# Two output projections with other banks and another written order, token statistics first, rotation tables on VectorE, in a two-layer hybrid decoder trunk

## The chip, the core and the metric

The kernel runs on one core of a Trainium2 chip. The core has TensorE (matmuls, which write to the eight banks of PSUM), VectorE, ScalarE and GpSimd, each with an instruction queue of its own that it works off in order, and SyncE (SP), whose queue issues the DMA transfers. GpSimd does not touch PSUM in this kernel. The metric is the device time of one execution in microseconds, the median of the runs. All arithmetic is on the device; the host only lays out the weights and transposes the activations.

## The reference

Input `x` has 1024 tokens of width 1024; there are two layers, each a mixer with a residual and a gated MLP with a residual. Cut to what matters:

```python
def reference(x, ...):
    h = x
    for layer in range(2):
        hn = rms_norm(h, mix_norm_g[layer])
        h = h + (even_mixer if layer == 0 else odd_mixer)(hn, ...)
        h = h + conv_ffn(rms_norm(h, ffn_norm_g[layer]), ...)
    return h

def even_mixer(hn, w_in, q_gain, k_gain, ret_gain, w_out):
    sb_q, sb_k, sb_v, r_q, r_k, r_v, r_g = split(hn @ w_in)
    out_a = stick_breaking_attention(rms_norm(heads(sb_q), q_gain), rms_norm(heads(sb_k), k_gain), heads(sb_v))
    ret = retention_chunkwise(rope(heads(r_q)), rope(heads(r_k)), heads(r_v))
    out_b = from_heads(rms_norm(ret, ret_gain)) * silu(r_g)
    return concatenate([out_a, out_b]) @ w_out

def odd_mixer(hn, w_in, w_alpha, b_alpha, out_gain, w_out):
    g_q, g_k, g_v, g_r, g_a = split(hn @ w_in)
    o = gla_chunked(g_q, g_k, g_v, log_sigmoid(g_a @ w_alpha + b_alpha) / 16)
    return (from_heads(rms_norm(o, out_gain)) * silu(g_r)) @ w_out
```

## The kernel before

Activations are kept transposed: eight tiles of 128 features x 1024 tokens. Every float32 operand of a large matmul is split into a high part (a ScalarE cast to the type that TensorE takes, `hi`) and a low part (the rest, `lo`, a subtraction on VectorE or GpSimd), and a product is three matmuls: hi x hi, hi x lo, lo x hi.

**Start.** `norm_end` makes 1/rms of the tokens from the sums of squares: twice as rows (`pn`, `self.rstd`, 512 tokens each, in the PSUM banks `st` and `O`) and once by token (`pt`, `self.rstd_tok`, 8 columns, in the bank `st`), each time with `rsqrt` (two ScalarE and three VectorE steps; L206 to L210). The first projection (queries and keys of the first head pair) and the values run meanwhile on TensorE; `sb_qk` scales them by the tokens' 1/rms, transposes them into the bank `st` (L587) and splits them (`split`, L541 and L546). The rotation tables `cos` and `sin` are loaded and multiplied by 1/rms on GpSimd (L895, L896).

**Even mixer.** Four rounds `p` of attention over head pairs are woven with projection units (`weave`, `work`): the next pair's queries and keys, a raw gate, values. `work` loads and splits the weight parts of a unit, part of them ahead during the unit before. VectorE, ScalarE and GpSimd keep the written order there (`manual_schedule`); TensorE's order, and that of any engine not named, is made by the framework's planner from its own costs. `issue_after(i)` keeps instructions behind instruction `i` of their engine.

**Output projections.** Each multiplies the concatenated heads `cat` (eight tiles) by a 1024 x 1024 matrix with Winograd's form of Strassen's scheme: for two blocks `p` of output features at a time, seven products, run in the order 1, 2, 3, 6, 7, 5, 4, each of 2 blocks x 4 tiles `c` x 3 matmuls = 24 matmuls of 128x512. After the first two blocks (with all the preparation of the right operands) come the other two blocks, another seven products with the right operands kept. The left operands are made from the weights by `out_left` in that order (11, 12, 12', s2, 21, 11', 22): sums on GpSimd (L294), cast on ScalarE (L71), subtraction (L73). The right operands 1, 2 and 3 are blocks of `cat` (`out_hi` L361, `out_lo` L367, the latter on GpSimd); 6, 7, 5 and 4 are mixes that `out_sums` makes tile by tile in two PSUM banks (a copy L440, two VectorE steps, a cast each L437 and a subtraction each L438, two VectorE steps more, again casts and subtractions). `out_group` runs the products into PSUM pairs `x`, `y`, `w`, `z` and adds them to the residual on VectorE (`sums`, L479).

In the even projection the last tile of `cat` is the gated one: `gate` multiplies a raw gate product by 1/rms, applies Silu, and multiplies tile 7 (L816 to L820). In the odd one, the last four gate blocks are the last seven products of `project_pair` (12 matmuls each, L1016 to L1018); `gla_gates` finishes each with three exponentials and logarithms, and `end()` (L1402) multiplies the result into `cat`.

Of the kernel before, what the change touches and what calls it, by code (L numbers as in the profile page):

```python
# [11 lines left out]
F32 = mybir.dt.float32  # L12
# [15 lines left out]
class Trunk:  # L28
# [219 lines left out]
    def norm_end(self, tok, second="O", parts=None):  # L248
        nc = self.nc
        self.rstd = self.cp.tile([P, T], F32, tag="rstd", name="rstd", bufs=1)  # L250
# [15 lines left out]
        if tok:  # L266
            ps = self.stat("pt")
            for tb in range(NC):
                nc.tensor.matmul(ps[:, tb:tb + 1], self.ssum[tb // 4][:, tb % 4 * P:(tb % 4 + 1) * P],
                                 self.ones_d[:, 0:1], start=True, stop=True)  # L270
            self.rstd_tok = self.cp.tile([P, NC], F32, tag="rstdt", name="rstdt", bufs=1)
            tmp = self.np_.tile([P, NC], F32, tag="ntmpt", name="ntmpt", bufs=1)
            self.rsqrt(self.rstd_tok, ps[:, :NC], tmp)
# [106 lines left out]
    def out_first(self, cat, res, norm, mm, gate):  # L380
# [17 lines left out]
        self.sums = [None] * 4  # L398
        with tc.manual_schedule(engines=self.MANUAL):
# [28 lines left out]
    def out_sums(self, cat, c, banks):  # L428

        t1, t2 = HALVES  # L430
        x, y = cat[c], cat[c + 4]

        def split(k, x):
            if k not in self.right[c]:
                self.right[c][k] = self.op(self.slot[c, k])
            hi, lo = self.right[c][k]
            self.nc.scalar.copy(hi, x)  # L437
            self.nc.vector.tensor_tensor(lo, x, hi.bitcast(F32), op=ALU.subtract)  # L438

        self.nc.scalar.activation(banks[0], x[:, t2], AF.Copy, scale=-1.0)  # L440
        yield
        yield from self.sums_psum((x[:, t1], x[:, t2], y[:, t1], y[:, t2]), (1.0, None, 1.0), banks, split)

    def out_group(self, ds, ops, h, res, part, cs=range(4), third=False):
# [7 lines left out]
        def product(bank, k):  # L452
            lefts = [next(o) for o in ops]
            start = (bank, 0) not in banks
            if start:
                for p in range(2):
                    if third and bank in third:
# [3 lines left out]
            order = [(p, c) for c in cs for p in range(2)] if part and (k == 1 or third and k in (2, 3, 6)) else \  # L461
                [(p, c) for p in range(2) for c in cs]
            for p, c in order:
                ps = banks[bank, p]
                (hi, lo), (bh, bl) = lefts[p], self.right[c][k]
                w = slice(c * P, (c + 1) * P)
                nc.tensor.matmul(ps, hi[:, w], bh, start=(start and c == cs[0]), stop=False, skip_group_check=True)  # L467
                nc.tensor.matmul(ps, hi[:, w], bl, start=False, stop=False, skip_group_check=True)  # L468
                nc.tensor.matmul(ps, lo[:, w], bh, start=False, stop=(c == cs[-1]), skip_group_check=True)  # L469
# [14 lines left out]
        if third:  # L484
            product("y", 2)
            yield
            product("w", 3)
            sums("11", "x", False)
            yield
            sums("11", "y", True)  # L490
            yield
            product("x", 6)
            yield
            sums("12", "w", False)
            yield
            product("z", 7)
# [33 lines left out]
    def sb_qk(self, pool, begin=None):  # L530
# [6 lines left out]
        def split(st, s, ts, key):  # L537
# [4 lines left out]
            for hd in range(2):  # L542
# [3 lines left out]
                nc.vector.scalar_tensor_tensor(low, st[own], gain[own], t.bitcast(F32), op0=ALU.mult, op1=ALU.subtract)  # L546
# [259 lines left out]
    def gate(self, cat, res, pool, ps, mm):  # L806
# [3 lines left out]
        u = [None, None]  # L810

        def evac(half, step):
            s = HALVES[half]
            if step == 0:
                t = pool.tile([P, 512], F32, tag="e0", name="e0", bufs=2)
                nc.vector.tensor_tensor(t, ps[half], self.rstd[:, s], op=ALU.mult)  # L816
                u[half] = t
                return nc.scalar.activation(t, t, AF.Silu).ins
            else:
                return nc.vector.tensor_tensor(cat[7][:, s], cat[7][:, s], u[half], op=ALU.mult).ins  # L820
# [16 lines left out]
    def even_mixer(self, pss, res):  # L837
# [14 lines left out]
        with tc.tile_pool(name="lp", bufs=1, reuse_waits="tile") as self.lp, \  # L852
                tc.tile_pool(name="com", bufs=1, reuse_waits="tile") as com:
            self.mixer_constants(com)
            with tc.tile_pool(name="sb", bufs=1, reuse_waits="tile") as pool:
# [31 lines left out]
                for _ in self.work([work], [a["we_t"][8]]):  # L887
                    pass
# [272 lines left out]
    def gla_gates(self, h, o, pool, s2, later=None):  # L1161
# [3 lines left out]
        def fin(block, x):  # L1165
# [10 lines left out]
            else:  # L1176
                tag = {"22": "p7", "21": "p2"}.get(block, "p")
# [992 lines left out]
```

## Time and profile before

| | |
|---|---|
| runs | 2362.7, 2361.07, 2355.01 us; median 2361.07 |
| profiled execution | 2358.64 us, its span 2356.8 us |
| TensorE busy | 2288.6 us (97%), 11672 matmuls |
| VectorE busy | 1516.9 us (64%) |
| GpSimd busy | 1411.2 us (60%) |
| ScalarE busy | 1122.0 us (48%) |
| mean granted TensorE clock | 0.991 |

The span runs from the first to the last instruction; the execution's own time is 1.84 us longer. Matmuls are pipelined: a record of 0.40 us for 128x512 columns starts 0.23 us after the one before. Idle time of an engine costs only what TensorE, or what comes last, loses by it.

### The profile page before, as it was taken

To read this page: it belongs to the slowest core of one execution; us is meant where nothing else is said; L and a number is where in the kernel's file an instruction comes from. 1 tells how busy PE (TensorE), PEld (TensorE's weight loads), DVE (VectorE), ACT (ScalarE), POOL (GpSimd) and SP (SyncE) were. 2 spreads that over 40 slices of the span, in tenths; PEclk is the share of its full clock that TensorE was granted. 3 is DMA by queue.
4 is the path that set the end of the run, shared out by engine and by line. 5 is a ranking of instruction groups with operands and counts; after the bars stand their busy time and mean duration, and the time that the engine had idled before them with its cause. 6 is when DMAs were issued, how large, how long until landed. Compare 5 with 4: busy or idle time off the path is not lost. (4 is left out here: it accounts for less than half of the span.)

```text
span 2356.8 us, 33097 instructions
## 1 busy us (share of the span) xinstructions
PE 2288.6 (97%) x11672; PEld 1868.6 (79%) x11672; DVE 1516.9 (64%) x2306; ACT 1122.0 (48%) x2030; POOL 1411.2 (60%) x1086
## 2 busy tenths in 40 slices
PE   9999999998999999999999899997999999999999
PEld 8887886886778888887888777985778888887887
DVE  7668668467976666664337876457886666665334
ACT  6445444245665555552225556355575555553221
POOL 2312314247677777757867574547677777767774
PEclk9999999998999999999999999998999999999999
DMA  4010001012334343449863122232333434339973
GB/s 165 28 37 19 24 23 38 31 62 65 111 139 152 143 152 143 153 166 357 303 218 115 51 72 85 73 114 70 134 133 127 170 126 170 126 147 349 319 241 112
DMA packets 141542, 310.25 MB, mean 132 GB/s; under 512 B 16224, under 2 KB 16608, under 8 KB 141376
## 3 DMA queue, kind: packets, MB, share of 16 engines
q1 hardware_dynamic: 141376, 308.14, 37.2%
q8 instruction: 92, 1.51, 0.3%
q14 instruction: 74, 0.61, 0.1%
HBM read 209.51 MB, written 98.57 MB: 131 GB/s over the span
## 5 line engine op out<-in xcount | busy, mean ns | idle before, releaser
L73 POOL TENSOR_TENSOR wl<-wr,wh 128x512 fp32r<-128x512 f32 x499 | 659.6, 1326 | 522.9 <-ACT wh L71 492.7
L71 ACT CAST wh<-wr 128x512 fp32r<-128x512 f32 x536 | 330.0, 622 | 521.2 <-PE up L1609 189.8
L1608 PE MATMUL up<-op,wh 128*128 128x512 f32 x1232 | 488.0, 396 | 4.8 <-DVE h L479 2.1
L1609 PE MATMUL up<-op,wh 128*128 128x512 f32 x1232 | 487.4, 396 | 0.0
L1610 PE MATMUL up<-op,wl 128*128 128x512 f32 x1232 | 487.1, 396 | 0.0
L1773 DVE TENSOR_TENSOR h<-dn,h 128x512 f32<-128x512 f32 x224 | 153.8, 691 | 248.7 <-PE dn L1769 247.4
L1608 PEld LDWEIGHTS up<-op,wh 128*128 128x128 f32 x1232 | 231.5, 188 | 64.0 <-ACT u L1641 2.8
L1609 PEld LDWEIGHTS up<-op,wh 128*128 128x128 f32 x1232 | 231.5, 188 | 55.7
L1610 PEld LDWEIGHTS up<-op,wl 128*128 128x128 f32 x1232 | 231.5, 188 | 55.7
L1769 PE MATMUL dn<-op,wl 128*128 128x512 f32 x616 | 243.9, 396 | 0.3 <-POOL wl L73 0.3
L1768 PE MATMUL dn<-op,wh 128*128 128x512 f32 x616 | 243.7, 396 | 0.0
L1767 PE MATMUL dn<-op,wh 128*128 128x512 f32 x616 | 242.8, 396 | 0.0
L162 PE MATMUL pv<-wh,xhi 128*128 128x256 f32 x512 | 152.2, 298 | 0.8 <-ACT xhi L243 0.8
L163 PE MATMUL pv<-wl,xhi 128*128 128x256 f32 x512 | 144.6, 283 | 1.1 <-POOL wl L73 1.0
L164 PE MATMUL pv<-wh,xlo 128*128 128x256 f32 x512 | 143.7, 282 | 1.2 <-DVE xlo L244 1.1
L1769 PEld LDWEIGHTS dn<-op,wl 128*128 128x128 f32 x616 | 115.7, 188 | 28.8 <-POOL wl L73 1.1
L1767 PEld LDWEIGHTS dn<-op,wh 128*128 128x128 f32 x616 | 115.7, 188 | 28.6 <-DVE g L1614 0.4
L1768 PEld LDWEIGHTS dn<-op,wh 128*128 128x128 f32 x616 | 115.8, 188 | 27.8
L627 DVE TENSOR_TENSOR_SCAN r<-r,zeros 128x512 f32<-128x512 f32 (+3 forms) x96 | 103.4, 1078 | 26.7 <-ACT r L620 22.4
L1614 DVE TENSOR_TENSOR up<-up,p 128x512 f32<-128x512 f32 x88 | 61.5, 699 | 81.9 <-PE up L1610 81.9
L467 PE MATMUL out<-op,wh 128*128 128x512 f32 x224 | 91.1, 409 | 15.3 <-ACT op L361 8.7
L162 PEld LDWEIGHTS pv<-wh,xhi 128*128 128x128 f32 x512 | 97.0, 190 | 9.6 <-issue 7.6
(354 smaller groups left out, 5043.7 us busy)
## 6 DMA issues: line engine op xcount, KB each, us to landing
b<-put SPq DMA_DIRECT2D x154, 512.0 KB, 2.6
op<-b SPq DMA_DIRECT2D x308, 256.0 KB, 5.3
wr<-in_wup_dram SPq DMA_DIRECT2D x176, 256.0 KB, 2.6
wr<-in_wdn_dram SPq DMA_DIRECT2D x44, 256.0 KB, 3.7
wr<-in_we_v_dram SPq DMA_DIRECT2D x32, 256.0 KB, 2.8
wr<-in_wod_t_dram SPq DMA_DIRECT2D x32, 256.0 KB, 2.6
wr<-in_we_t_dram SPq DMA_DIRECT2D x24, 256.0 KB, 2.6
a<-in_wdn_dram SPq DMA_DIRECT2D x24, 256.0 KB, 4.7
```

What stands on the lines that cost most here:

```text
L71: self.last_hi = nc.scalar.copy(hi, x).ins
L73: self.last_lo = (engine or nc.gpsimd).tensor_tensor(lo, x, hi.bitcast(F32), op=ALU.subtract).ins
L162: nc.tensor.matmul(o, self.xhi[c][:, t], hi[:, w], start=start, stop=False, skip_group_check=True)
L163: nc.tensor.matmul(o, self.xhi[c][:, t], lo[:, w], start=False, stop=False, skip_group_check=True)
L164: nc.tensor.matmul(o, self.xlo[c][:, t], hi[:, w], start=False, stop=(c == NC - 1), skip_group_check=True)
L1608: nc.tensor.matmul(ps, hi[:, w], bh, start=(start and c == 0), stop=False, skip_group_check=True)
L1609: nc.tensor.matmul(ps, hi[:, w], bl, start=False, stop=False, skip_group_check=True)
L1610: nc.tensor.matmul(ps, lo[:, w], bh, start=False, stop=(c == 3), skip_group_check=True)
L1767: nc.tensor.matmul(ps, wh[:, w], gh, start=start, stop=False, skip_group_check=True)
L1768: nc.tensor.matmul(ps, wh[:, w], gl, start=False, stop=False, skip_group_check=True)
L1769: nc.tensor.matmul(ps, wl[:, w], gh, start=False, stop=end, skip_group_check=True)
L1773: nc.vector.tensor_tensor(h[d][:, s], ps, h[d][:, s], op=ALU.add)
```

## The change

Six edits.

1. `norm_end`: the statistics by token are made first, before the two rows.
2. `even_mixer`: in the first round (`p == 0`) the unit of the next queries and keys comes ahead of the raw gate, as in the other rounds; the two rotation tables are multiplied on VectorE, behind the last split of the first queries and keys.
3. `gate`: the gate is finished in its PSUM bank (no SBUF tile); the product with tile 7 of `cat` stays in PSUM, from where ScalarE casts the right operands 2 and 3 of that tile, VectorE subtracts their low parts, and ScalarE copies the tile back.
4. `out_group`: with `third`, `x` has the banks `z`, `y` the banks `T`, `w` the banks `pj`, and only `z` the banks `O` and `st` (before, `w` and `z` shared these two in the even projection; in the odd one `w` had them and `z` had `T`). Products 1, 2 and 3 run all hi x hi first, then hi x lo, then lo x hi; product 2 takes three tiles so and then the last one. The sums of block 12 stand ahead of product 6, and there are more steps to interleave with.
5. `out_sums` is four pieces (`first`, `second`, `low`, `high`) instead of a generator; `out_first`, `layer` and `odd_mixer` write out a new order with them. The even projection's mixes are in `O`/`st` (tiles 0 and 1), `T` (2) and `pj` (3); the odd one's in `O`/`st` (0, 1 and 3) and `T` (2).
6. `gla_gates`: the last exponential of the four late blocks stays in its PSUM bank.

```diff
@@ norm_end
+        if tok:
+            ps = self.stat("pt")
...
+            self.rsqrt(self.rstd_tok, ps[:, :NC], tmp)
         self.rstd = self.cp.tile([P, T], F32, tag="rstd", name="rstd", bufs=1)
...
-        if tok:
...
@@ out_first
-        group = self.out_group((0, 1), self.lefts, self.h, res, True, third="wz")
+        group = self.out_group((0, 1), self.lefts, self.h, res, True, third=True)
...
+            for c in range(3):
+                H(3, c)
             self.sums[0] = self.out_sums(cat, 0, [self.stat("mx", "O"), self.stat("mx", "st")])
-            next(self.sums[0])
             gate(0, 0)
-            self.last_silu = gate(1, 0)
+            gate(1, 0)
             for c in range(3):
                 L(2, c, g)
             next(group)
-            next(self.sums[0])
-            gate(0, 1)
-            gate(1, 1)
-            H(2, 3)
-            L(2, 3, g)
+            first, _, low, _ = self.sums[0]
+            first(6)
+            low(6)
+            for half, k in ((0, 2), (1, 3)):
+                x = gate(half, 1)
+                hi, _ = self.right[3][k]
+                nc.scalar.copy(hi, x)
+                if half == 0:
+                    for c in range(3):
+                        L(3, c, g)
+                self.last[half] = x
+            for half, k in ((0, 2), (1, 3)):
+                hi, lo = self.right[3][k]
+                v.tensor_tensor(lo, self.last[half], hi.bitcast(F32), op=ALU.subtract)
+                nc.scalar.copy(cat[7][:, HALVES[half]], self.last[half])
             next(group)
@@ out_sums
+        bank = {6: a, 7: b, 5: b, 4: a}
+        copy(a, b12)
+        def low(*ks):
+            for k in ks:
+                hi, lo = self.right[c][k]
+                v.tensor_tensor(lo, bank[k], hi.bitcast(F32), op=ALU.subtract)
+        def high(*ks):
...
+                copy(self.right[c][k][0], bank[k])
+        def first(*ks):
+            v.tensor_tensor(b, b22, a, op=ALU.subtract)
+            v.tensor_tensor(a, b11, b, op=ALU.add)
+            high(*(ks or (6, 7)))
+        def second():
+            v.tensor_tensor(b, b22, a, op=ALU.subtract)
+            v.tensor_tensor(a, b21, a, op=ALU.subtract)
+            high(5, 4)
@@ out_group
-                        banks[bank, p] = self.pj("out", {"x": "z", "y": "T", "z": "T" if third else "pj"}[bank])
+                        banks[bank, p] = self.pj("out", {"x": "z", "y": "T", "z": "pj", "w": "pj"}[bank])
...
+                order = [(p, c, m) for some in ((cs[:3], cs[3:]) if k == 2 else (cs,))
+                         for m in range(3) for c in some for p in range(2)]
...
@@ gate
             if step == 0:
-                t = pool.tile([P, 512], F32, tag="e0", name="e0", bufs=2)
-                nc.vector.tensor_tensor(t, ps[half], self.rstd[:, s], op=ALU.mult)
...
+                nc.vector.tensor_tensor(x, x, self.rstd[:, s], op=ALU.mult)
+                nc.scalar.activation(x, x, AF.Silu)
             else:
-                return nc.vector.tensor_tensor(cat[7][:, s], cat[7][:, s], u[half], op=ALU.mult).ins
+                nc.vector.tensor_tensor(x, x, cat[7][:, s], op=ALU.mult)
@@ even_mixer
-                for _ in self.work([work], [a["we_t"][8]]):
+                for _ in self.work([work], [a["we_v"][5, 0], a["we_v"][5, 1]]):
...
-                nc.gpsimd.tensor_tensor(self.cos, self.cos, self.rstd, op=ALU.mult)
-                nc.gpsimd.tensor_tensor(self.sin, self.sin, self.rstd, op=ALU.mult)
                 for p in range(4):
                     self.flush()
+                    if p == 0:
+                        with tc.issue_after(self.last_split):
+                            for t in (self.cos, self.sin):
+                                nc.vector.tensor_tensor(t, t, self.rstd, op=ALU.mult)
...
-                        units.insert(p == 0, u)
+                        units.insert(0, u)
@@ gla_gates
-                tag = {"22": "p7", "21": "p2"}.get(block, "p")
-                t = pool.tile([P, 512], F32, tag=tag, name=tag, bufs=1)
-                nc.scalar.activation(t, x, AF.Exp, scale=-1.0)
-                later.append((c[:, s], t))
+                nc.scalar.activation(x, x, AF.Exp, scale=-1.0)
+                later.append((c[:, s], x))
@@ layer (the even projection; s: the four out_sums)
+                high(7)
                 make()
+                low(7)
+                second()
+                low(5, 4)
                 next(group)
+                s[1] = self.out_sums(cat, 1, [self.stat("mx", "O"), self.stat("mx", "st")])
+                s[1][0]()
+                next(group)
+                s[1][2](6)
                 next(group)
                 s[2] = self.out_sums(cat, 2, [self.pj("mx", "T") for _ in range(2)])
+                s[2][0]()
+                make()
+                s[1][2](7)
+                s[2][2](6)
+                next(group)
                 s[3] = self.out_sums(cat, 3, [self.pj("mx") for _ in range(2)])
+                s[3][0]()
+                s[2][2](7)
+                s[3][2](6)
                 next(group)
+                s[1][1]()
+                s[3][2](7)
                 make()
+                s[1][2](5, 4)
                 next(group)
+                s[2][1]()
+                s[3][1]()
+                s[2][2](5, 4)
+                s[3][2](5, 4)
                 next(group)
```

The new order of the odd projection is of the same kind: the third gate product's copy and the first mix stand ahead of the four casts of operand 1; the mixes follow in the order of tiles 0, 1, 3, 2, the first two sums of the products between the third and the fourth mix, and the casts of the left operand `s2` behind the fourth.

## Rows read from the trace of the kernel before

**Rows 1.** The page, section 1: busy us (share of the span) xinstructions.

```profile
PE 2288.6 (97%) x11672; PEld 1868.6 (79%) x11672; DVE 1516.9 (64%) x2306; ACT 1122.0 (48%) x2030; POOL 1411.2 (60%) x1086
```

**Rows 2.** TensorE's waits, whole span: us in total, times, longest.

```profile
PE out L467 <- ACT op L361: 8.7, 1, 8.7
...
PE out L468 <- POOL op L367: 5.7, 3, 4.7
...
PE out L467 <- ACT wh L71: 5.7, 1, 5.7
```

**Rows 3.** Timeline, TensorE, start: start us, us, line, operation [idle before <-releaser].

```profile
30.53 1.88 PE L254 MATMUL pn<-ssum,ones_d 128*128 128x512 f32 x4
...
35.65 1.95 PE L269 MATMUL pt<-ones_d,ssum 128*128 128x1 f32 x16
...
47.36 0.63 PE L587 MATMUL st<-con,e 128*128 128x128 f32 x2 [2.72 <-issue]
...
49.49 0.41 PE L163 MATMUL pv<-wl,xhi 128*128 128x256 f32 x1
...
50.77 0.31 PE L163 MATMUL pv<-wl,xhi 128*128 128x256 f32 x1
```

**Rows 4.** Timeline, VectorE and GpSimd, start.

```profile
34.91 0.68 DVE L210 SCALAR_TENSOR_TENSOR rstd<-pn,rstd 128x512 f32<-128x512 f32 x1
...
38.37 1.05 DVE L209 SCALAR_TENSOR_TENSOR ntmpt<-ntmpt,rstdt 128x8 f32<-128x8 f32 x1
...
39.45 2.32 DVE L210 SCALAR_TENSOR_TENSOR rstdt<-ntmpt,rstdt 128x8 f32<-128x8 f32 x1
...
37.00 2.40 POOL L895 TENSOR_TENSOR cat<-cat,rstd 128x1024 f32<-128x1024 f32 x1 [0.94 <-DVE rstd L210]
```

**Rows 5.** Timeline, around the first attention: VectorE, then TensorE.

```profile
62.46 1.51 DVE L546 SCALAR_TENSOR_TENSOR qk<-st,cols,qk 64x512 fp32r<-64x512 f32 x2 [2.24 <-ACT qk L541]
...
130.47 0.44 PE L587 MATMUL st<-con,e 128*128 128x128 f32 x2 [2.48 <-DVE e L577]
```

**Rows 6.** Timeline, TensorE, even output projection.

```profile
550.08 0.80 PE L468 MATMUL out<-op,wh 128*128 128x512 f32 x1 [4.71 <-POOL op L367]
...
550.67 0.63 PE L469 MATMUL out<-op,wl 128*128 128x512 f32 x1
...
576.40 0.79 PE L467 MATMUL out<-op,wh 128*128 128x512 f32 x1 [5.66 <-ACT wh L71]
```

**Rows 7.** Timeline, VectorE, GpSimd and ScalarE, even output projection.

```profile
540.72 3.24 DVE L820 TENSOR_TENSOR cat<-cat,e 128x512 f32<-128x512 f32 x2
...
548.77 2.50 POOL L367 TENSOR_TENSOR op<-cat,op 128x512 fp32r<-128x512 f32 x2
...
570.78 0.69 DVE L479 TENSOR_TENSOR rr<-out,rr 128x512 f32<-128x512 f32 x1 [2.10 <-PE out L469]
...
575.73 3.21 ACT L71 CAST wh<-wr 128x512 fp32r<-128x512 f32 x6
```

**Rows 8.** Timeline, TensorE and VectorE, odd output projection.

```profile
1603.79 0.74 PE L469 MATMUL out<-op,wl 128*128 128x512 f32 x1 [2.64 <-POOL wl L73]
...
1627.65 0.80 PE L467 MATMUL out<-op,wh 128*128 128x512 f32 x1 [8.74 <-ACT op L361]
...
1634.91 0.50 PE L467 MATMUL out<-op,wh 128*128 128x512 f32 x1 [0.85 <-DVE op L438]
...
1701.97 0.40 PE L469 MATMUL out<-op,wl 128*128 128x512 f32 x1
...
1611.03 4.50 DVE L1402 TENSOR_TENSOR go<-go,p 128x512 f32<-128x512 f32 x1
```

**Rows 9.** Single lines, whole span: min/median/max ns, first and last start.

```profile
L438 DVE TENSOR_TENSOR op<-mx,op x32: 681/691/693, 540.1 to 1643.1; 128x512 fp32r<-128x512 f32 x32
...
L71 ACT CAST wh<-wr x536: 598/621/677, 4.4 to 2336.2; 128x512 fp32r<-128x512 f32 x179
...
L1138 DVE TENSOR_TENSOR ek<-ek,mid x4: 1216/1225/1226, 1352.4 to 1394.5; 128x1024 f32<-128x1024 f32 x4
```

More of the change, by code (lines that the diff above doesn't have):

```diff
@@ L431, in out_sums @@
         x, y = cat[c], cat[c + 4]
[L433 to L442, printed above, removed]
+        b11, b12, b21, b22 = x[:, t1], x[:, t2], y[:, t1], y[:, t2]
+        a, b = banks
+        v, copy = self.nc.vector, self.nc.scalar.copy
+        bank = {6: a, 7: b, 5: b, 4: a}
[5 more added lines that the diff above has]
+        def high(*ks):
+            for k in ks:
+                if k not in self.right[c]:
+                    self.right[c][k] = self.op(self.slot[c, k])
+                copy(self.right[c][k][0], bank[k])
[7 more added lines that the diff above has]
+            high(5, 4)
+        return first, second, low, high
     def out_group(self, ds, ops, h, res, part, cs=range(4), third=False):
@@ L456, in product @@
                 for p in range(2):
-                    if third and bank in third:
+                    if third and bank == "z":
                         banks[bank, p] = self.stat("out", ("O", "st")[p])
                     else:
-                        banks[bank, p] = self.pj("out", {"x": "z", "y": "T", "z": "T" if third else "pj"}[bank])
[L461 to L469, printed above, removed]
+                        banks[bank, p] = self.pj("out", {"x": "z", "y": "T", "z": "pj", "w": "pj"}[bank])
+            if not third or k not in (1, 2, 3):
+                order = [(p, c, m) for c in cs for p in range(2) for m in range(3)] if third and k == 6 else \
+                    [(p, c, m) for p in range(2) for c in cs for m in range(3)]
+            else:
+                order = [(p, c, m) for some in ((cs[:3], cs[3:]) if k == 2 else (cs,))
+                         for m in range(3) for c in some for p in range(2)]
+            for p, c, m in order:
+                left, right = lefts[p][m == 2], self.right[c][k][m == 1]
+                nc.tensor.matmul(banks[bank, p], left[:, c * P:(c + 1) * P], right,
+                                 start=(start and c == cs[0] and m == 0), stop=(c == cs[-1] and m == 2),
+                                 skip_group_check=True)
         def sums(block, bank, end):
@@ L1423, in odd_mixer @@
         self.h = []
-        group = self.out_group((0, 1), [pull(i) for i in range(2)], self.h, res, True, (0, 1, 3, 2), "w")
+        group = self.out_group((0, 1), [pull(i) for i in range(2)], self.h, res, True, (0, 1, 3, 2), True)
         with tc.manual_schedule(engines={mybir.EngineType.DVE, mybir.EngineType.Activation}):
+            product()
+            product()
+            c0 = chain(0)
             product()
@@ L1429, in odd_mixer @@
                 hi(1, c)
-            product()
-            c0 = chain(0)
-            next(c0)
-            next(c0)
+            c0[0]()
             for c in range(4):
@@ L1437, in odd_mixer @@
             product()
-            next(c0)
+            c0[2](6)
+            product()
+            c0[2](7)
+            c0[1]()
+            end()
             split(2, 0)
@@ L1441, in odd_mixer @@
             product()
+            end()
             left()
-            rest(c0)
-            product()
+            c0[2](5, 4)
             end()
-            c1 = chain(1)
-            next(c1)
-            next(c1)
-            split(3, 0)
-            product()
-            end()
-            next(c1)
-            rest(c1)
-            split(3, 1)
-            end()
-            c3 = chain(3)
-            next(c3)
-            next(group)
             split(2, 3)
@@ L1461, in odd_mixer @@
             split(2, 2)
-            next(c3)
+            next(group)
+            c1 = chain(1)
+            c1[0]()
+            split(3, 0)
+            split(3, 1)
+            c1[2](6, 7)
+            c1[1]()
             left()
+            c1[2](5, 4)
             split(3, 3)
```

78 lines of the change are left out of this document (31 added, 47 removed).

## The prediction

> **What bounds the kernel now.** I read the page first: TensorE is busy for 2288.6 of 2356.8 us [rows 1], so everything but TensorE's idle time (68 us) and the operations that it runs at its lower clock is out of reach of this change, which leaves the number of matmuls as it is. Then TensorE's waits over the whole span: the three longest are single waits, all in the two output projections, on casts of ScalarE or subtractions of GpSimd [rows 2]. Then the timelines around them. The reader is to see three things.
>
> At the start (the first 65 us) the token statistics `pt` run only at 35.65, 5 us after the row statistics `pn`, because they want the bank `st`, which VectorE reads until 34.91 + 0.68 = 35.59 [rows 3, 4]. Two of the three tiny VectorE steps that follow take 1.05 and 2.32 us for 8 elements a row while GpSimd scales the rotation table [rows 4]; the values' 1/rms is there at 39.45 + 2.32 = 41.8. TensorE has run dry at 44.64 and waits 2.72 us; behind it the records read 0.41 instead of 0.28 until 50.77, half speed for 3.4 us, which loses 1.7. In sum 4.4 us.
>
> In the even projection (534 to 590) the long waits are 4.71 and 5.66 us, each followed by matmuls at the lower level: 13 records and 7 records of 0.63 instead of 0.40, at 0.19 each 2.5 and 1.4 us [rows 6]. In sum 14.3 us. The first wait ends with a subtraction that GpSimd began at 548.77, though its input was multiplied at 540.72 + 3.24 = 543.96: it stood behind other work [rows 7]. The second ends with a cast at 575.73, behind VectorE's sums, which had waited at 570.78 for TensorE's own product 7 [rows 7]: the queues hold each other up.
>
> In the odd projection the waits are 2.64, 8.74 and 0.85; 8 and 11 slow records behind the first two lose another 3.6 us: 15.8 in sum [rows 8]. Here VectorE loses 4.50 us to a single product of two SBUF tiles [rows 8]; the subtraction of the same size with an input in PSUM takes 0.68 to 0.69 in all 32 records [rows 9].
>
> **The change, part by part.** The sum is made against the profiled execution's 2358.64 us (span 2356.8 and 1.84 around it); the runs' median, 2361.07, is 2.4 above it.
>
> *1/rms by token first.* `pt` takes the place of `pn` at 30.53: 1.95 us of matmuls, two ScalarE and three VectorE steps on 8 columns, some 1 us when nothing holds them: the tokens' 1/rms is there by about 33.6 instead of 41.8. The four ScalarE and six VectorE steps of the row statistics (6 x 0.69 = 4.1) now stand among the work that led from 41.8 to the first transposition at 47.36, 5.6 us: 33.6 + 5.6 + 4.1 = 43.3, before TensorE runs dry at 44.64. So the 4.4 us go: **-4.4**. Bounds: all of it, or nothing, if the row statistics' steps held that chain a second time (4.1 more, 47.4).
>
> *Second queries and keys first; tables on VectorE.* Nothing is added to TensorE. The unit needs four weight parts, of which two can be made ahead; the other two are subtracted on VectorE behind the first step of the attention. That step stands behind the two tables, which wait for the last split of the first queries and keys (end 62.46 + 1.51 = 63.97 now, some 3.5 earlier then) and take 2 x 1.23 (the row for 128x1024 [rows 9]). TensorE has 12 matmuls of the unit (1.4 us) and the scores meanwhile, and then waits for a subtraction some 5 us after the split: I take **+2** (0 if TensorE's values last longer, +5 if the tables are held as L1402 was, by 3.8 us, and TensorE finds 0.8 more to do). The tables hide behind nothing there but that wait. In return the unit's last transpositions, for which TensorE waits 2.48 us at 130.47 with the values already running [rows 5], come 16 steps of the weave earlier: **-2** (0 to -2.5). GpSimd loses 2 x 2.40 us; that was no bound. On SP's queue two more weight loads of 256 KB pass ahead of the tables, which are multiplied some 25 us later; between 30 and 65 us nothing on TensorE waits for a load.
>
> VectorE's steps on 8 columns at 38.37 and 39.45 read two SBUF tiles and were long while GpSimd ran [rows 4]. The Trainium skill, "SBUF — State Buffer", section "Who interferes with whom", says that a VectorE instruction with two SBUF inputs contends with a GpSimd instruction that reads SBUF, and that one with at most one SBUF input doesn't. The trace agrees on both sides: 4.50 us for L1402, 0.69 for L438 [rows 8, 9]. By that rule the moved tables (two SBUF inputs) can be held in their turn by GpSimd's copies of the keys or its weight parts, and the +2 would be about +5: rival (d).
>
> *Even projection.* Two multiplications by the Silu gate now work on PSUM with one SBUF input: 2 x 0.69 instead of 3.24, -1.9 us on VectorE. The last two low parts go from GpSimd to VectorE (+2 steps), ScalarE gets two copies more. From 540.7: multiplication 0.7, five ScalarE steps in a row (two casts, two copies, one cast, 0.53 apart by the six casts in 3.21 us [rows 7]) 2.7; product 2's last operand is there at 543.5, not 550.0. TensorE, which stood at 545.37 four matmuls before the end of product 2, goes on: product 3 ends at about 551.9 (24 matmuls at 0.2337: 288 from 1634.91 to 1702.2 [rows 8], so 5.6 a product). Then it wants the cast of the left operand `s2`, which stands on ScalarE behind the third mix. Path on from 544.1, with 0.69 for a VectorE step [rows 9] and 0.6 for a ScalarE step (0.62 [rows 9]): three VectorE steps 2.1, cast 0.6, subtraction 0.7, copy 0.6, two mixing steps 1.4, five VectorE steps (sums and one low part) 3.4, copy 0.6 (it starts after the fourth of them: -0.7), two mixing steps 1.4, two casts and the cast of `s2` 1.7: 555.9. TensorE waits some 4 us and then runs slow for the price of the second wait above, 1.4 to 2.5: product 6 ends at 563.5, product 7 at 569.1 to 570.2. VectorE has 25 steps between 553.3 and the sums that let product 5 start: 17.3, so 570.6. Product 5 starts at 570.6 instead of 576.40 and not at the lower clock: 5.8 + 1.4, **-7**. Bounds: 0 (the wait only moves) and -14.3 (all waiting gone).
>
> *Odd projection.* The exponentials stay in PSUM, so the four last multiplications have one SBUF input: 4.50 falls to 0.69 (-3.8), the other three 0.5 in mean. The copy of the third gate product now stands ahead of four casts; I count nothing for it. Without the 2.64, and with the gate products first, TensorE ends its 24 gate matmuls at 1603.79 - 2.64 + 5.6 = 1606.8 and product 1 at 1611.7. The last gate block takes two VectorE, three ScalarE and one VectorE step more: 1610.7. The path from there, with the same prices: copy and mix 2.0; cast, four VectorE steps, cast, two steps 5.4; copy, mix, cast 2.6; two low parts and three sums 3.5; copy, mix, two casts and the cast of `s2` 3.7: 1627.9. By then product 3 is done, unless GpSimd is late (25 operations at 1.25 [rows 7], 31 us, of some 36 that it has). Product 6 starts at 1627.9, loses 1.5 to the lower clock, and products 6, 7, 5, 4 end at 1651.8. Now they end at 1702.2 - 7 x 5.6 = 1663.0. -11.2; since GpSimd's and TensorE's orders are not written out there, I take **-10**. Bounds: 0 and -15.8.
>
> Sum: -4.4 + 2 - 2 - 7 - 10 = -21.4, so 2337.2 against the profile's time and 2339.6 against the median: I forecast 2339.
>
> **Rivals.** (a) *A planned order eats half.* TensorE's order is the planner's. It put five matmuls of product 1 ahead of 24 ready gate matmuls (the 2.64 at 1603.79, 4 us with the slow records [rows 8]), and a subtraction on GpSimd behind others (548.77 [rows 7]). Four such places cost 14 us: 2353. Against it: the new order runs all high parts first, which puts off what GpSimd makes. (b) *The waits only move.* If product 6's left cast came at 563 and 1638 (7 and 11 us after my times), each projection would be where it was, and the start alone leaves 2354 + 2 - 2 + 2.4 for the median, 2357. The new order does put that cast behind three of four mixes; that speaks for it. (c) *Slower.* VectorE's sums wait for TensorE (2.10 at 570.78), and behind them stands what TensorE wants next. Sums of products 1 to 3 are now in the middle of the mixes. Were TensorE to wait ahead of each of the 12 products of the first halves of both projections, at 4 us with 2 slow, the two would cost 72 instead of 30.1: +42, less 4.4, 2399. It decides from 3.5 us a product on (12 x 3.5 = 30.1 + 4.4 + 7). Against it: the sums find their products done by 3 us or more on my paths. (d) *The tables are held and the first attention starts late:* +5 instead of +2, and no gain at 130: 2339 + 5 = 2344. For it speaks that both inputs lie in SBUF, against it that GpSimd has two short copies there. (e) *Better:* product 6 finds its operands, both projections lose under 3 us: 2324.
>
> **Chances.** Forecast, 2330 to 2349: 0.48. (d), in the same range: 0.12. (a), up to 2354: 0.13. (e), below 2330: 0.09. (b): 0.11. (c): 0.07. What a measurement can tell from no change is about 0.3%, 7 us: faster is below 2354. Faster 0.48 + 0.12 + 0.13 + 0.09 = 0.82, no change 0.11, slower 0.07. From 2326 to 2354 lies about 0.79.
>
> **What would show it.** `pt` before 33 and no wait of 2 us between 44 and 48; no VectorE step on 8 columns over 0.5 us there. A wait of 1 to 3 us at the first unit of the first attention, none near 130. In the even projection no wait on L367 over 1 us, one of about 4 us ahead of product 6, product 5 starting 5 us or more earlier, counted from product 1. In the odd one the four multiplications at 0.69, and one wait of up to 4 us ahead of product 6. Wrong would be: waits in front of product 3 (the `pj` banks not free), a GpSimd row last in both projections, or more than 40 us of slow records.

## The result and the profile after

The changed kernel takes 2335.5 us (median of 4 runs, 2334.74 to 2336.99) against 2359.9 for the kernel before (4 runs): ratio 0.990, 95% interval 0.9882 to 0.9917. The forecast was 2339, range 2326 to 2354. The profiled span is 2335.2 us. One execution of one kernel further down (both left operands cast earlier) took 3463.71 us at a mean granted clock of 0.59, and its ratio leaves that execution out.

The page's first section: TensorE's busy time hardly changes, so the gain is idle time, and time at the lower clock, not matmuls [rows 1].

```profile
PE 2285.6 (98%) x11672; PEld 1865.0 (80%) x11672; DVE 1507.9 (65%) x2310; ACT 1123.5 (48%) x2032; POOL 1405.3 (60%) x1082
```

TensorE's waits over the whole span (total, times, longest). The single waits of 8.7, 4.7 and 5.7 us [rows 2] are gone. In the projections (`out`) three waits for GpSimd's low parts stay, one for a cast of a left operand, and small ones.

```profile
PE out L499 <- POOL op L367: 5.9, 3, 3.0
...
PE up L1642 <- DVE h L511: 3.0, 2, 1.5
...
PE out L499 <- ACT wh L71: 2.5, 1, 2.5
...
PE out L499 <- POOL wl L73: 0.8, 2, 0.6
```

The timeline of TensorE: the start and the first attention [rows 3, 5], the even projection [rows 6], the odd one [rows 8].

```profile
30.58 1.84 PE L253 MATMUL pt<-ones_d,ssum 128*128 128x1 f32 x16
...
43.52 0.44 PE L622 MATMUL st<-con,e 128*128 128x128 f32 x2
...
64.30 0.39 PE L163 MATMUL pv<-wl,xhi 128*128 128x256 f32 x1 [0.47 <-DVE wl L73]
...
118.10 0.39 PE L163 MATMUL pv<-wl,xhi 128*128 128x256 f32 x1 [1.00 <-POOL wl L73]
...
535.03 0.73 PE L499 MATMUL out<-op,wh 128*128 128x512 f32 x2 [0.51 <-POOL op L367]
...
551.34 0.74 PE L499 MATMUL out<-op,wh 128*128 128x512 f32 x2 [2.50 <-ACT wh L71]
...
564.92 0.63 PE L499 MATMUL out<-op,wh 128*128 128x512 f32 x2
...
1601.99 0.74 PE L499 MATMUL out<-op,wh 128*128 128x512 f32 x2 [2.97 <-POOL op L367]
...
1610.72 2.47 PE L499 MATMUL out<-op,wh 128*128 128x512 f32 x4 [2.38 <-POOL op L367]
...
1616.40 1.05 PE L499 MATMUL out<-op,wh 128*128 128x512 f32 x2
...
1678.97 0.40 PE L499 MATMUL out<-op,wl 128*128 128x512 f32 x1
1680.90 0.47 PE L1642 MATMUL up<-op,wh 128*128 128x512 f32 x1 [1.54 <-DVE h L511]
```

The reader sees `pt` first and the first transposition at 43.52 with no wait; 0.47 and 1.00 us in the first attention where 2.48 stood at 130.47; product 6 at 551.34 behind 2.50 us, product 5 at 564.92 behind none; in the odd projection two waits ahead of the last low parts of products 2 and 3, and none ahead of product 6 at 1616.40.

The other engines at the same places [rows 4, 7, 8]:

```profile
59.13 1.23 DVE L936 TENSOR_TENSOR cat<-cat,rstd 128x1024 f32<-128x1024 f32 x1
...
537.39 1.29 DVE L854 TENSOR_TENSOR pj<-pj,cat 128x512 f32<-128x512 f32 x2
...
562.79 1.87 DVE L511 TENSOR_TENSOR rr<-out,rr 128x512 f32<-128x512 f32 x3
...
1591.89 0.68 DVE L1437 TENSOR_TENSOR go<-go,pp 128x512 f32<-128x512 f32 x1
...
550.65 1.15 ACT L71 CAST wh<-wr 128x512 fp32r<-128x512 f32 x2
...
1614.96 1.15 ACT L71 CAST wh<-wr 128x512 fp32r<-128x512 f32 x2
...
1600.66 2.54 POOL L367 TENSOR_TENSOR op<-go,op 128x512 fp32r<-128x512 f32 x2
...
1609.38 2.53 POOL L367 TENSOR_TENSOR op<-go,op 128x512 fp32r<-128x512 f32 x2
```

By stage, from the starts of the same instructions in both timelines ("earlier" is before minus after; the last column is how much it grew since the row above):

| Start of | before | after | earlier | gained in the stage |
|---|---|---|---|---|
| an attention step in the last pair | 410.87 | 406.46 | 4.41 | 4.41 |
| product 1, even projection | 534.05 | 531.10 | 2.95 | -1.46 |
| first MLP | 630.52 | 616.93 | 13.59 | 10.64 |
| last gate statistics of the linear attention | 1590.85 | 1577.67 | 13.18 | -0.41 |
| last matmul, odd projection | 1701.97 | 1678.97 | 23.00 | 9.82 |
| second MLP | 1702.82 | 1680.90 | 21.92 | -1.08 |
| end | 2356.8 | 2335.2 | 21.6 | -0.3 |

### The profile page after: what moved, and what is told of

It is laid out like the page before. It is cut to its first block, busy times and chain, and to the rows that moved or that the text cites. A ratio compares the mean times of both kernels' runs of the same rounds, so it can differ in the third digit from the quotient of the medians.

```text
span 2335.2 us, 33112 instructions
## 1 busy us (share of the span) xinstructions
PE 2285.6 (98%) x11672; PEld 1865.0 (80%) x11672; DVE 1507.9 (65%) x2310; ACT 1123.5 (48%) x2032; POOL 1405.3 (60%) x1082
## 5 line engine op out<-in xcount | busy, mean ns | idle before, releaser
L499 PE MATMUL out<-op,wh 128*128 128x512 f32 x448 | 138.0, 403 | 8.4 <-POOL op L367 5.9
L499 PEld LDWEIGHTS out<-op,wh 128*128 128x128 f32 x448 | 84.9, 191 | 31.6 <-POOL op L367 8.1
```

The costliest lines, as they stand in the source:

```text
L499: nc.tensor.matmul(banks[bank, p], left[:, c * P:(c + 1) * P], right, start=(start and c == cs[0] and m == 0), stop=(c == cs[-1] and m == ...
```

## The experiments

Intervals of the ratio are mostly about 0.17% to either side, 4 us, so most of these runs are told apart by their traces. What a stage varies by itself: product 1 starts at 528.0 to 531.1 in the eight profiled executions that have the same instructions up to there; an even projection that is as in the changed kernel lasts 85.8 to 87.1 us to the first MLP (eight), an odd one 101.3 to 102.4 from the last gate statistics to its last matmul (eight).

For the start there is a narrower mark than product 1: the matmuls behind a wait of 1.70 us near 360, which stand ahead of the lower clock that moves product 1 (last section). In the same eight executions they start at 359.79 to 360.22. In order: the kernel before, the changed kernel, and the kernel before with the tables on VectorE (below).

```profile
364.20 1.39 PE L652 MATMUL O<-wt,v 128*64 128x128 f32 x14 [1.70 <-DVE r L626]
```

```profile
359.79 1.09 PE L687 MATMUL O<-wt,v 128*64 128x128 f32 x14 [1.70 <-DVE r L661]
```

```profile
359.97 1.67 PE L653 MATMUL O<-wt,v 128*64 128x128 f32 x14 [1.70 <-DVE r L627]
```

### Tokens first alone (kernel before)

```diff
 def norm_end(self, tok, ...):
+    if tok: (1/rms by token)
     self.rstd = ... (row statistics)
-    if tok: (1/rms by token)
```

> The kernel before with one edit: the 1/rms by token made first. Theory (the prediction's first term, which is charged to the order alone): the 4.4 us of the start go, the first scores start about 4 us earlier than at 64.70, no wait of 2 us between 44 and 49, about 2355.5. Rival (the order pays only together with the tables): the two multiplications of the rotation tables stay on GpSimd behind the row statistics, now from about 39 to 44 us, on top of the VectorE steps of 8 columns that stand at 40 to 45 in the changed kernel; several of these read two SBUF tiles and take 1 to 2.3 us instead of 0.16, TensorE runs dry again and the gain is 0 to 2 us: 2358 to 2360, first scores at 62.7 or later.

Measured: 2359.77 us, ratio 0.9999 (0.9990 to 1.0008); the mark at 364.76, product 1 at 534.6. TensorE, VectorE, GpSimd of this run, timeline:

```profile
46.72 0.44 PE L587 MATMUL st<-con,e 128*128 128x128 f32 x2 [3.19 <-DVE e L577]
...
41.16 1.84 DVE L565 TENSOR_SCALAR r<-r 128x8 f32<-128x8 f32 x1
...
43.52 1.80 DVE L208 SCALAR_TENSOR_TENSOR r<-r,r 128x8 f32<-128x8 f32 x1
...
40.58 2.40 POOL L895 TENSOR_TENSOR cat<-cat,rstd 128x1024 f32<-128x1024 f32 x1
42.94 2.35 POOL L896 TENSOR_TENSOR sin<-sin,rstd 128x1024 f32<-128x1024 f32 x1
```

Each of two VectorE steps on 8 columns ends when a table multiplication on GpSimd ends (41.16 + 1.84 = 43.00 against 42.98; 45.32 against 45.29). The rival holds: the order gains nothing while GpSimd has the tables. The step at 41.16 reads only one SBUF tile, and was held too (0.17 in the changed kernel).

### Tables back on GpSimd; tokens last; gate first (changed kernel, each undone alone)

```diff
-nc.vector.tensor_tensor(t, t, self.rstd, op=ALU.mult)   # behind last_split, both tables
+nc.gpsimd.tensor_tensor(...)                            # behind the loads, both tables
```

> The changed kernel with the two table multiplications back on GpSimd, where they were. Theory (VectorE's steps of 8 columns are held by GpSimd's tables): GpSimd runs them from about 39 to 44 us and the steps of 8 columns there take 1 us or more each; TensorE waits 1 to 3 us for the first transposition at 43.5, and 2 to 4.4 us of the start are lost: 2337.5 to 2340. Rival (nothing is held, the tables only cost the place they take): the step behind the split starts 2.5 us earlier on VectorE, the wait of 0.47 us at 64.30 goes, 2335.0.

The edit for tokens last is the first experiment's taken back, in the changed kernel.

> The changed kernel with the 1/rms by token made last again, the tables still on VectorE. Theory (the order is what pays): the wait of 2.7 us at about 47 us returns with its slow matmuls, 4.4 us, 2335.5 + 4.4 = 2339.9. Rival (the tables, once off GpSimd, free the same chain): the steps of 8 columns take 0.2 us in the old order too, the tokens' 1/rms is there at 35.65 + 1.95 + 1.3 = 38.9 instead of 41.8, the first transposition wants to start at 38.9 + 5.6 = 44.5, where TensorE runs dry at 44.6: under 1 us is lost, 2335.5 to 2336.5.

```diff
-units.insert(0, u);        work ahead: a["we_v"][5, 0], a["we_v"][5, 1]
+units.insert(p == 0, u);   work ahead: a["we_t"][8]
```

> The changed kernel with the first gate ahead of the second queries and keys again. Theory (the prediction's second term): the wait of 2.5 us near 126 to 130 returns, the waits of 0.47 us at 64.30 and 1.00 at 118.10 go, so it loses 1 to 2 us: 2336.5 to 2337.5. Rival (a wait near 130 is filled by the next stage anyway): no difference, 2335.5.

Measured, tables on GpSimd: 2340.01 us, 0.9917 (0.9897 to 0.9937); the mark at 364.23, 4.0 to 4.4 us late. The wait returns, with the same two long steps on VectorE (1.84, 1.79), as the theory has it:

```profile
46.84 0.44 PE L622 MATMUL st<-con,e 128*128 128x128 f32 x2 [3.19 <-DVE e L612]
```

Measured, tokens last: 2338.2 us, 0.9906 (0.9889 to 0.9923); the mark at 361.21, 1.0 to 1.4 us late. No wait stands at 45, so the theory fails, but the rival's "under 1 us" is a little short. The splits and the tables behind them come 1.2 us later on VectorE, and two of its weight parts are late instead of one:

```profile
64.79 0.38 PE L163 MATMUL pv<-wl,xhi 128*128 128x256 f32 x1 [0.81 <-DVE wl L73]
...
66.48 0.39 PE L163 MATMUL pv<-wl,xhi 128*128 128x256 f32 x1 [0.72 <-DVE wl L73]
```

Measured, gate first: 2336.75 us, 0.9903 (0.9887 to 0.992); the mark at 361.96, 1.7 to 2.2 us late. This row of its TensorE timeline is the wait that returns, as the theory has it:

```profile
127.02 0.59 PE L622 MATMUL st<-con,e 128*128 128x128 f32 x2 [2.49 <-DVE e L612]
```

Behind it the granted clock is 0.97 from 120 to 185 us. The kernel before and the one with the tables alone have the same wait (2.48, 2.47) and 1.00 there, so some 1.4 of the 1.7 to 2.2 us are this lower clock and not the order of the units (the last section has more such cases).

None of the three is told from the changed kernel by its time alone.

### Tables on VectorE alone (kernel before)

```diff
-nc.gpsimd.tensor_tensor(self.cos, ...), (self.sin, ...)
+with tc.issue_after(self.last_split): nc.vector.tensor_tensor(t, t, self.rstd, ...)
```

> The kernel before with one edit: the two table multiplications on VectorE behind the first split, instead of on GpSimd. Theory (formed from the first four runs: the start was lost to GpSimd's tables, not to the order of the statistics): the steps of 8 columns at 38 to 45 us take 0.15 to 0.2 us instead of up to 2.32, the wait of 2.72 us at 47.36 goes, the wait of 2.5 near 130 stays; 2 to 4.4 us faster, 2356 to 2358.5. Rival (tokens first and tables pay only together, as tokens first alone gained nothing): within 1 us of before, the wait at 47 still over 2 us.

Measured: 2359.42 us, 0.9991 (0.9977 to 1.0004; 12 runs from 2353.23 to 2364.07). By time it is not told from no change, and the median misses the theory's range. Its trace shows the start mended, with `pt` still last: the mark at 359.97 instead of 364.20, product 1 at 529.8 instead of 534.05.

```profile
44.98 0.38 PE L588 MATMUL st<-con,e 128*128 128x128 f32 x2
...
39.13 0.17 DVE L210 SCALAR_TENSOR_TENSOR rstdt<-ntmpt,rstdt 128x8 f32<-128x8 f32 x1
```

The step that took 2.32 us [rows 4] takes 0.17, and no wait stands before 44.98. This one edit brings the mark as early as the changed kernel has it (359.79 to 360.22): on top of it, tokens first and the new place of the gate together bring nothing that can be seen, though in the changed kernel taking back either alone costs 1.0 to 1.4 and 0.3 to 0.8 us.

### Exponentials in SBUF again (odd projection)

```diff
-nc.scalar.activation(x, x, AF.Exp, scale=-1.0);  later.append((c[:, s], x))
+nc.scalar.activation(t, x, AF.Exp, scale=-1.0);  later.append((c[:, s], t))   # t: SBUF tile
```

> The changed kernel with the exponentials of the last gate block written to SBUF tiles again, so that the four multiplications behind them read two SBUF tiles. Theory (the prediction's term of 3.8 + 1.5 us): GpSimd works without a break from 1584 to 1613, so one or more of the four take 1.5 to 4.5 us instead of 0.64 to 0.69; VectorE's chain to the mixes of the odd projection comes up to 5 us later, and the kernel is 2 to 5 us slower, 2337.5 to 2340.5. Rival (there is slack): VectorE stands idle for 1.46 us at 1596.9 and 2.28 at 1604.4 behind ScalarE, and TensorE waits for GpSimd there, not for VectorE; the delay is swallowed, 2335.5 to 2336.5.

Measured: 2337.76 us, 0.9902 (0.9887 to 0.9916); the odd projection lasts 103.5 us. VectorE's timeline, the last three of the four multiplications:

```profile
1592.21 1.70 DVE L1439 TENSOR_TENSOR go<-go,p 128x512 f32<-128x512 f32 x1
...
1595.04 3.49 DVE L1439 TENSOR_TENSOR go<-go,p 128x512 f32<-128x512 f32 x2
```

They lengthen as the theory says, by 0.3 + 1.0 + 2.2 us; the stage pays 1.1 to 2.2. The idle time behind them (1.46 us at 1596.9 in the changed kernel, none there now) swallows the rest.

### Four low parts from GpSimd to VectorE (odd projection)

```diff
 def split(k, c):
     hi(k, c)
-    lo(k, c, nc.gpsimd)
+    lo(k, c, nc.vector if c > 1 else nc.gpsimd)
```

> The changed kernel with four low parts of the odd projection (the third and fourth block's for products 2 and 3) moved from GpSimd to VectorE. GpSimd is busy without a break from 1584 to 1613 and TensorE waits for it at 1601.99 (2.97) and 1610.72 (2.38). Theory (the prediction's: product 6 comes when ScalarE casts s2, whatever stands before): both waits go, product 3 is done 5 us or more earlier, and TensorE waits instead ahead of product 6, whose left operand is cast at 1615.0 behind the last mix: net -1 to +1 us, 2334.5 to 2336.5. Rival (GpSimd is the limit of this stage): product 6 starts 5 to 7 us earlier too, 2329 to 2330.5.

Measured: 2341.39 us, 0.9915 (0.9900 to 0.9930); the odd projection lasts 108.6 us. Neither expectation. Timelines of TensorE, VectorE, ScalarE and GpSimd:

```profile
1602.31 1.22 PE L499 MATMUL out<-op,wh 128*128 128x512 f32 x2 [4.12 <-DVE op L367]
...
1621.70 1.22 PE L499 MATMUL out<-op,wh 128*128 128x512 f32 x2 [6.22 <-ACT wh L71]
...
1596.51 5.75 DVE L367 TENSOR_TENSOR op<-go,op 128x512 fp32r<-128x512 f32 x1 [1.05 <-ACT op L361]
...
1621.01 1.15 ACT L71 CAST wh<-wr 128x512 fp32r<-128x512 f32 x2
...
1596.77 2.50 POOL L73 TENSOR_TENSOR wl<-wr,wh 128x512 fp32r<-128x512 f32 x2
1599.24 2.47 POOL L294 TENSOR_TENSOR wr<-wr 128x512 f32<-128x512 f32 x2
```

One subtraction of two SBUF tiles on VectorE takes 5.75 us: until GpSimd's four instructions, which follow each other without a gap, are through at 1601.71. With GpSimd idle, the next one takes 0.68. The whole chain of mixes behind it is 6 us later, and the cast of `s2`, at 1621.01 instead of 1614.96, makes product 6 wait 6.22: that half of the theory, that product 6 hangs on this cast, is seen here.

### Four low parts left out (odd projection)

The low parts of the right operand of product 1 are left out; its high part is used in their place, so the matmuls are the same.

```diff
-for c in range(4): lo(1, c, nc.gpsimd)
+for c in range(4): self.right[c][1] = (self.right[c][1][0],) * 2
```

> The changed kernel without the four low parts of the right operand of product 1 in the odd projection (the high part is used twice; GpSimd has 5.1 us less to do from 1584 on, on the same matmuls). Theory (two limits lie close together): GpSimd's waits of 2.97 and 2.38 go, but product 6 cannot start before ScalarE casts s2 at about 1615, behind the last mix; TensorE waits there instead, 4 to 5 us, and the time falls by 0.5 to 2 us only, 2333.5 to 2335. Rival (GpSimd alone is the limit): the mixes follow TensorE's sums, all of it moves forward, 4 to 6 us faster, 2329.5 to 2331.5.

Measured: 2335.83 us, 0.9887 (0.9870 to 0.9905), against 2335.92 for the changed kernel on the same chip; the odd projection lasts 100.9 us. TensorE's timeline:

```profile
1599.87 0.73 PE L499 MATMUL out<-op,wh 128*128 128x512 f32 x2 [2.37 <-POOL op L367]
...
1608.59 2.46 PE L499 MATMUL out<-op,wh 128*128 128x512 f32 x4 [2.39 <-POOL op L367]
```

Both waits stay, so both expectations fail: counted from the last gate statistics, 5.1 us less work on GpSimd make the low part that product 2 waits for 0.6 us earlier (1.3 against the second execution of the changed kernel). In this trace GpSimd now stands idle for 2.19, 1.89 and 0.32 us behind ScalarE's casts, and the low parts still stand behind two left parts and a sum in its queue. That it is this order which counts was not tried.

### Last low parts on GpSimd again (even projection)

```diff
-v.tensor_tensor(lo, self.last[half], hi, op=ALU.subtract)          # from PSUM
 nc.scalar.copy(cat[7][:, HALVES[half]], self.last[half])
+g.tensor_tensor(lo, cat[7][:, HALVES[half]], hi, op=ALU.subtract)  # from the copy
```

> The changed kernel with the last two low parts of the even projection (the gate's block) made by GpSimd again, from the copy in SBUF. They stand behind ten subtractions and two weight parts, at 545.0 to 547.6 instead of 539.2 to 540.5. TensorE wants the first at 541.9 and waits 4 to 5 us in product 2. Theory (one wait hides in the next): product 6 waits 2.50 us for its left operand anyway, and that chain does not stand behind the low parts; of the 5 us (and 1.5 of slow matmuls) some 3 are swallowed, so +1.5 to +3, 2337 to 2338.5. Rival (waits add up): +5 to +6.5, 2340.5 to 2342, with the wait of 2.5 ahead of product 6 still there.

Measured: 2337.57 us, 0.9901 (0.9886 to 0.9916); the even projection lasts 89.2 us, 2.1 to 3.4 more. TensorE's timeline:

```profile
543.19 1.22 PE L499 MATMUL out<-op,wh 128*128 128x512 f32 x2 [3.27 <-POOL op L435]
...
559.19 0.71 PE L499 MATMUL out<-op,wh 128*128 128x512 f32 x2 [1.52 <-DVE op L453]
```

A wait of 3.27 us comes ahead, the one of 2.50 ahead of product 6 is gone, one of 1.52 follows: one wait hides in the next, as the theory has it.

### Left operands cast earlier (even projection)

```diff
+make()          # s2's cast
 s[2][0]()
-make()
 ...
+make()          # the next left operand's cast (second run only)
 s[1][1]()
 s[3][2](7)
-make()
```

> The changed kernel with the cast of the left operand s2 of the even projection issued on ScalarE one place earlier, ahead of the third mix's casts instead of behind them: at about 548.1 to 549.2 instead of 550.65 to 551.8. Theory (the prediction's: this cast is what product 6 waits for): the wait of 2.50 us goes, product 6 starts at about 549.2; then the low part of the fourth block for product 6, made by VectorE at about 555, is wanted at 553.5 and costs 1 to 1.7; with fewer slow matmuls -1 to -2.5, 2333 to 2334.5. Rival (another operand is as late): the wait only moves to that low part or to GpSimd's part of s2, 2335.5.

Measured: 2335.28 us, 0.9889 (0.9873 to 0.9906); the even projection lasts 85.0 us. TensorE's timeline:

```profile
547.09 0.50 PE L499 MATMUL out<-op,wl 128*128 128x512 f32 x1 [0.35 <-POOL wl L73]
...
554.96 1.20 PE L499 MATMUL out<-op,wh 128*128 128x512 f32 x4 [1.65 <-ACT wh L71]
```

The cast was what product 6 waited for: that wait is gone. But 1.65 us come back one product on, at another operand than I had named, and the median lies at the rival's 2335.5, not in the theory's range.

> The changed kernel with both late casts of left operands in the even projection one place earlier on ScalarE: s2's ahead of the third mix's casts (as in the run before) and the next one's ahead of the third mix's second half. Theory: in the run with one cast moved the wait of 2.50 us ahead of product 6 became 1.65 ahead of the next product, whose cast stood at 553.77 behind mixes though its operand was there at 552.2; moved, it comes at 552 and that wait falls under 0.6; the projection is 2 us shorter than in the changed kernel, 2333 to 2334. Rival (VectorE's mixes are now the limit): the wait moves again, to the operands of product 5, 2335 to 2336.

Measured: 2333.64 us, 0.9876 (0.9857 to 0.9895). The even projection lasts 85.0 us again, so the second cast gains nothing; the wait ahead of product 7, up to 554.58, is now 1.20 us, on a low part of VectorE's. In kind this is the rival (VectorE's mixes are the limit), one product earlier than it had it. This is the lowest median of all kernels, but its interval overlaps that of the changed kernel.

### The changed kernel again

> The changed kernel once more, on the same chip as the three others, as their reference. 2335.5; ratio 0.990. The lower clock behind the wait of 2.27 us at 406 to 409 us, which only the first profile of this kernel shows out of six kernels with the same wait, is expected gone (theory: it falls by chance, and the end of the first attention comes 1.4 us earlier) or there again (rival: it belongs to this program).

Measured: 2335.92 us, 0.9889 (0.9870 to 0.9908); profiled span 2338.4. The slow matmuls behind the wait at 405 to 408 us are there again, those at 360 are not; more in the last section. (The expectation had overlooked a case: the run with four low parts on VectorE has the slow matmuls behind that wait too.) In the odd projection one wait now stands where the first execution had none, ahead of product 6:

```profile
1619.31 0.73 PE L499 MATMUL out<-op,wh 128*128 128x512 f32 x2 [1.06 <-ACT wh L71]
```

## Why the prediction was right, and where not

**Start, -4.4: right in size, wrong in cause.** The first transposition was put at 43.3 and came at 43.52; the 4.41 us are there at 406.46. But the step that failed is "GpSimd loses 2 x 2.40 us; that was no bound". Those two multiplications were the bound: they held VectorE's steps on 8 columns. The first run and the run with the tables back show it from both sides, and with the tables alone the start is mended with the old order: 4.23 of the 4.41 us. The rows for it had been read [rows 4], and only their place in the order was costed.

**Second queries and keys, +2 and -2.** The wait meant by -2 is right: 2.48 us gone, and back as 2.49 with the gate first; without the lower clock behind it that run loses some 0.3 to 0.8 us only. The +2 was too much: 0.47 us at 64.30, since nothing held the tables (1.23 us, GpSimd idle), and 1.00 at 118.10 on a GpSimd weight part, which I had not seen. Rival (d) fell.

**Even projection, -7: measured -10.6.** Counted with the start 2.95 earlier, the times on the path came out: product 2's last operand at 543.4 (543.5), product 6 at 554.3 behind 2.50 us (555.9 behind 4). The term that was mis-sized is VectorE's run of "25 steps: 17.3" to the sums ahead of product 5: steps that follow each other on one engine start 0.60 us apart, not 0.69 (22 steps from 550.92 to 564.66: 0.62 each). 25 x 0.62 = 15.5, so 570.6 becomes 568.8; with the start 1.6 earlier, 567.2. The sums are through at 564.66 + 2.95 = 567.6, and product 5 starts at 567.9 behind no wait. That is 2.7 of the 3.6 us. Most of the rest is the slow matmuls behind the old wait: product 5 took 7.56 us before and takes 5.60 now, 1.96 less, where 1.4 was counted.

**Odd projection, -10: measured -9.8, with the waits elsewhere.** The four multiplications take 0.64 to 0.68, and with SBUF inputs 1.0 to 1.8 each. Product 6 was put at 1627.9 and starts at 1616.40 + 13.18 = 1629.6. But TensorE did not wait there: 2.97 and 2.38 us came before, on GpSimd ("unless GpSimd is late" in the prediction). In the second execution 1.06 us stand ahead of product 6 on the left cast, and in the first the casts of `s2` end at 1614.96 + 1.15 = 1616.11, 0.3 us before product 6, so the two limits lie within about 1 us of each other. Rival (a) was thus right in kind, but by these times it can have cost little, because product 6 could hardly have started earlier. No run shows the stage without those two waits: where they were attacked, they stayed or VectorE's chain came late.

**Given back.** 1.46 us between 406 and 531 (a lower clock, below), and 1.08 at the second MLP, where the wait for VectorE's last sum grew from 0.45 to 1.54. Neither had a term.

**A sum.** Rival (e)'s 2324 is 2358.64 - 4.4 - 14.3 - 15.8: no waiting at all in the projections, and without the 2.4 up to the median that the forecast has. Its own words, under 3 us lost in both, give 2326.5 to 2332.5, which overlaps the forecast's 2330 to 2349.

## What to carry to other kernels

When VectorE has short steps that read SBUF on the critical path, look at what GpSimd runs in those microseconds: moving 4.8 us of GpSimd work mended what a better order of VectorE's own steps could not. Operands left in PSUM keep VectorE's steps at 0.69 us under a busy GpSimd; a step with two SBUF inputs moved there to relieve GpSimd can cost more than it relieves (5.75 us for one). When waits stand in a row, do not add them up: the 3.27 us ahead in the even projection cost 2.1 to 3.4 with their slow matmuls, because the 2.50 behind went.

## What the runs showed of the hardware

VectorE can be held over several GpSimd instructions: 5.75 us instead of 0.68, across four that follow without a gap, to 0.55 us behind their end. The 4.50 us before [rows 8] also end 0.55 us behind a run of four on GpSimd (1609.90 to 1614.98). The Trainium skill, "SBUF — State Buffer", section "Who interferes with whom", says that whoever issues first has the shared ports for the whole instruction and the other is fully blocked. The traces agree for one instruction (1.84 us, ending with GpSimd's table); the 5.75 us show that the next instruction of GpSimd can also go ahead of the VectorE step that is waiting. It does not always: with the exponentials in SBUF the four VectorE steps came through in 1.0 to 1.8 us each under an unbroken run of GpSimd, and GpSimd lost time too, up to 3.41 us for a pair that takes 2.54 in the changed kernel. What decides between the two was not tried.

```profile
1596.27 3.41 POOL L73 TENSOR_TENSOR wl<-wr,wh 128x512 fp32r<-128x512 f32 x2
```

The prediction gave that section's rule for a step with at most one SBUF input without its condition, "outside the 2-port perf modes". The held step of 1.84 us reads one SBUF tile, so one input alone did not spare it; whether it ran in such a mode the profile does not show.

TensorE's granted clock falls behind the same wait in one execution and not in another. Two stretches with the same instructions and the same waits (1.70 us before 359.79, 2.27 us before 409.16 in the changed kernel), first the changed kernel, then the run with exponentials in SBUF; busy times by engine, then the granted clock, DMA share, GB/s:

```profile
354.00:366.00 12.00, 10.30 (x55) 7.50 (x53) 8.69 (x15) 3.54 (x9) 2.55 (x2) 0.86 0.15 45
400.00:415.00 15.00, 12.73 (x84) 9.68 (x84) 11.31 (x14) 6.43 (x10) 9.67 (x7) 0.89 0.33 107
```

```profile
354.00:366.00 12.00, 10.30 (x67) 7.35 (x67) 10.14 (x16) 4.65 (x11) 2.55 (x2) 1.00 0.15 45
400.00:415.00 15.00, 12.65 (x92) 9.71 (x92) 10.68 (x13) 5.59 (x9) 8.32 (x6) 1.00 0.34 105
```

Means of 0.86 and 0.89 are stretches at 1.2 GHz among others at 2.4. Of eight executions with the same instructions up to there, one had the first fall and three the second. The changed kernel's two executions differ in the first (0.86 and 1.00); both have the second, as has one of the six others, so for the second alone chance is likely but not shown. Product 1 starts at 528.0 without either and at 531.1 with both: some 1.5 us a fall, and a gain below that is not read from one profile.
